# Two-layer diffusion backbone: the last feed-forward weights through the rings, the norm's products in the tokens' place

## The chip, the cores and the metric

One core of a Trainium2 chip runs the whole forward pass in one launch. The metric is the device time in microseconds of one execution; the median of three runs of the kernel before is 2040.7 us (2039.86 to 2040.83). The engines in the rows are TensorE (PE for the matmuls, PEld for its weight loads), VectorE (DVE), ScalarE (ACT), GpSimd (POOL), and SyncE (SP), which starts the transfers.

## What is computed

512 latent tokens and 256 context tokens of 1024 channels pass two layers. Context tokens go through the same steps as latent ones in layer 0. Each layer mixes tokens in two branches (attention over a window of neighbours, and grouped attention over all), then has a gated feed-forward part of 2816 hidden channels. Layer 1, the last, updates latent tokens alone. Cut to what matters:

```python
DEPTH = 2; SEQ = 512; CTX_LEN = 256; D_MODEL = 1024; D_FF = 2816
def swiglu(h, w_in, w_out):
    a, u = jnp.split(h @ w_in, 2, axis=-1)
    return (jax.nn.silu(a) * u) @ w_out
for l in range(DEPTH):
    ...
    h = modulate(rms_norm(x, norm1[l]), sh1, sc1)
    na_q, na_k, na_v, gq, gk, gv, ga, gb = jnp.split(h @ w_in[l], IN_SPLITS, axis=-1)
    ...
    x = x + g1 * branch_merge(ya, yb, ga, gb, w_pa[l], w_pb[l], w_o[l])
    h2 = modulate(rms_norm(x, norm2[l]), sh2, sc2)
    x = x + g2 * swiglu(h2, w_ffn_in[l], w_ffn_out[l])
    ...
return rms_norm(x, final_norm)
```

## The kernel before, in words

Channels lie on the 128 partitions, tokens on the free axis: `x[k]` is channel block k of 8. All is fp32 in value, and each matmul is done as three in fp32r: high part by high part, high by low, low by high (`steps`, L377). So each block of weights is loaded raw (`wr`), rounded on ACT to its high part `wh` (L362), and DVE or POOL subtracts to get the low part `wl` (L364). The ring of raw buffers has four places, those of high and low parts three each; beside them is a pool of 45 slots of 768 columns, "s", for tokens, hidden blocks and much else.

The feed-forward part does most of its products in a scheme of seven in place of eight (`qu`, `qv`, `qc`, L1691). Its last six hidden blocks (`LAST`) come at its end in the plain way: for each of two groups of tokens, for each of eight output blocks j, 6 x 3 = 18 matmuls into `po` (L377), the residual (DVE, L1570: `x[j]` plus gate times `po`), the square of it for the next norm (ACT, L474 for the first and L477) and the addition of squares (DVE, L478). The groups are tokens 0 to 512 and 512 to 768 in layer 0, 0 to 256 and 256 to 512 in layer 1. The hidden block that ends last is `ph`/`pl` (L1777 and L1778). Here the eight blocks of weights, high and low, are kept in 16 of the 45 slots (`kept`) through both groups.

After a group, `done` makes its norm: `st` (L489, sum over partitions on TensorE), `rs` (L498 on DVE, L499 the power on POOL), `rb` (L502, spread to all partitions). In layer 0 `following` then writes the group's tokens to DRAM (`xd`, L1941; layer 1 reads them back for its residual) and makes layer 1's normed input: for each k a product `u` (DVE, L522), its high part `h` (ACT, L523), its low part `hl` (DVE, L524). Context tokens are left for `late_norm`, inside layer 1's mixing. In layer 1 `final` scales and writes the output (L1950 to L1953).

The framework's scheduler sets the order on every engine from these calls; TensorE's is written by hand only in the mixing and in the seven-products part. In mixing, a planner with a clock of its own puts projections among the attention: `PLAN` gives their order as `fill` (`gq` queries, `gb` gates, `nq`, `nk`, `nv` queries, keys and values of the window branch), and until its clock passes `quiet`, a few low parts and rotary products go to DVE rather than POOL. Layer 1 starts with the keys and first queries of the grouped branch, for which two kept blocks are converted in L1263 and L1264 (`kh`, `kl`).

Of the kernel before, what the change touches and what calls it, by code (L numbers as in the profile page):

```python
# [12 lines left out]
F32 = mybir.dt.float32  # L13
# [7 lines left out]
P = 128  # L21
D = 1024
KB = D // P
S = 512
CTX = 256
T = S + CTX
DEPTH = 2
# [6 lines left out]
CHUNK, LAST = 4, 6  # L34
# [8 lines left out]
for _n in ORDER:  # L43
    for _j in range(COLS[_n][1]):
# [25 lines left out]
               "gb4 nk1 gb5 nq2 nk2 nv1 nq3 nk3 gb6 gb7"),  # L70
         early=0.9, reserve=8, hop=0.14, move=3.5, soon=0.5, keep=2,
         busy=12, ctx=0.0, vat=(1, 1), load=2, qt=2, rx=2, slow=(1.1, 1.2, 1), banks="gst", lead=(2, 1, 2), quiet=0.0, spared=0),
    dict(fill=("gq1 gb0 nq0 nv0 gq2 gb1 gq3 gb2 nq1 nk0 gb3",
               "nk1 nk2 nq2 nv1 nk3 gb4 nq3 gb5 gb6 gb7"),
         early=0.8, reserve=2, hop=0.2, move=3, soon=0, keep=2,
         busy=2, ctx=1, vat=(1, 1), load=2.5, qt=2, rx=1, slow=(1, 1, 1), banks="tsg", lead=(2, 2, 1), quiet=18.0, spared=2),
]


# [14 lines left out]
def drain(steps):  # L94

    while True:
        try:
            next(steps)
        except StopIteration as e:
            return e.value  # L100
# [166 lines left out]
class Ops:  # L267
# [6 lines left out]
    def add(self, engine, cost, run, args, after, urgency):  # L274
        self.ops.append((engine, cost, run, args, after, urgency))
        return len(self.ops) - 1
# [51 lines left out]
class Trunk:  # L328
# [27 lines left out]
    def weight(self, src, cols, eng=None, pool=None):  # L356

        nc = self.nc
        raw = self.raw(src, cols)
        tile = lambda tag: (pool or self.wpool).tile([P, cols], F32R, tag="we" if pool else tag, name=self.name(tag))  # L360
        hi = tile("wh")
        nc.scalar.activation(hi, raw, AF.Copy)  # L362
        lo = tile("wl")
        (eng or nc.gpsimd).tensor_tensor(lo, raw, hi[:].bitcast(F32), op=ALU.subtract)  # L364
        if self.flow:
            self.go(("a", cols), ("v" if eng else "g", cols), at=self.flow.clock + self.plan["load"])
        return hi, lo
# [138 lines left out]
    def modulated(self, l, i, x, acc, a, b, h, pool):  # L506

        rb = self.rstd(acc, b - a, pool)
        for k in range(KB):
            self.modulate(l, i, k, x, rb, a, b, h, pool)  # L510

    def modulate(self, l, i, k, x, rb, a, b, h, pool):
        nc = self.nc
        s = int(a >= S)
        if len(h[0]) == k:
            h[0].append(self.slot("h", F32R))
            h[1].append(self.slot("hl", F32R))
        hi, lo = h[0][k], h[1][k]
        u = pool.tile([P, S], F32, tag="u", name=self.name("u"))[:, : b - a]
        g = self.A[l][i][:, s, k : k + 1]  # L520
        sh = self.mod[l][:, s, 24 * i + k : 24 * i + k + 1]
        nc.vector.scalar_tensor_tensor(u, x[k][:, a:b], g, rb[:, : b - a], op0=ALU.mult, op1=ALU.mult)  # L522
        nc.scalar.activation(hi[:, a:b], u, AF.Identity, bias=sh)  # L523
        nc.vector.scalar_tensor_tensor(  # L524
            lo[:, a:b], u, sh, hi[:, a:b].bitcast(F32), op0=ALU.add, op1=ALU.subtract)
# [742 lines left out]
    def late_norm(self, l, h, at):  # L1268

        nc, flow = self.nc, self.flow  # L1270
        x, acc = at.rest
        nb = CTX // P
        yield Until(max(flow.clock + self.plan["ctx"], flow.ring("t")))
        st = self.rstd(acc, CTX, None, True)
        yield nb * 2 * PASS
        t = self.go(("v", nb))
        flow.took("t", t)
        yield Until(self.go(("p", nb + 3), at=t))
        yield Until(flow.ring("t"))
        rb = self.spread(st, nb, Alias(self.small, "hr"))  # L1280
        yield nb * 2 * PASS
        end = flow.clock
        for k in range(KB):
            self.modulate(l, 0, k, x, rb, S, T, h, Alias(self.att, "p"))
            first = self.go(("v", CTX), at=end if k == 0 else None)
            end = self.go(("a", CTX), ("v", CTX), at=first)
        flow.took("t", first)
        self.ready["h"] = end + 2.0
# [450 lines left out]
    def ffn(self, l, right, late, x, spans, groups, nh, done, pool, beside):  # L1739
        nc, d = self.nc, self.d  # L1740
# [80 lines left out]
            beside.pop(0)[1]()  # L1821

        chunk = (FB - LAST) // CHUNK
        kept, slots = [], _Bufs(None, {}, dict(we=self.spool))
        for a, b in groups:
            acc = None
            for j in range(KB):
                if a == 0:
                    kept.append(self.weight(d["wfo"][l, j, :, chunk * CHUNK * P :], LAST * P, nc.vector, slots))
                w = kept[j]  # L1830
                ps = self.ps("a", "po")[:, : b - a]
                drain(self.steps(ps, w, second[chunk], a, b, LAST))
                self.residual(l, 1, ps, x, j, a, b)
                if l == DEPTH - 1 and b == groups[-1][1] and j >= KB - 2:

                    acc = [acc] if j == KB - 2 else acc
                    acc.append(pool.tile([P, S], F32, tag="sq", name=self.name("sq")))
                    nc.scalar.activation(acc[-1][:, : b - a], x[j][:, a:b], AF.Square)
                else:
                    acc = self.square(x[j], a, b, pool, acc)  # L1840
            done(acc, a, b)

    def run(self):
        nc, tc, d = self.nc, self.tc, self.d
        joint = [(0, S), (S, T)]
        self.flow = None
        with (
# [9 lines left out]
            h = ([], [])  # L1857
            with (
# [5 lines left out]
                pool = _Bufs(pool_, dict(rs=1, row=3, more=1, wr=AHEAD), dict(qt=self.spool))  # L1864
                self.constants(cpool)
                at = Front()
                spare = _Bufs(None, {}, dict(qt=self.spool))
                todo = self.prologue(0, h, joint, spare, at)
                self.start(h, pool, todo)
            xd = [self.dpool.tile([P, S], F32, name=f"xd{k}") for k in range(KB)]  # L1870
            for l in range(DEPTH):
                last = l == DEPTH - 1
                spans = joint[:1] if last else joint
                groups = [(0, 256), (256, 512)] if last else joint
# [4 lines left out]
                with (  # L1879
# [2 lines left out]
                    ExitStack() as stack,  # L1882
                ):
                    self.psum = dict(n=psn, a=psa)
                    slots = dict(acc=self.spool, sq=self.spool, u=self.spool)
                    rows, conds = [], stack.enter_context(tc.tile_pool(name=f"c{l}", bufs=1, reuse_waits="tile"))

                    def one(of, n):
# [8 lines left out]
                    with tc.tile_pool(name=f"m{l}", bufs=1, reuse_waits="tile") as pool_:  # L1897
                        pool = _Bufs(pool_, dict(rs=2, qt=5), slots)
# [4 lines left out]
                        x = []  # L1903
# [26 lines left out]
                    h = ([], [])  # L1930
                    at = Front()
                    with tc.tile_pool(name=f"f{l}", bufs=1, reuse_waits="tile") as pool_:
                        own = dict(we=4) if last else {}
                        pool = _Bufs(pool_, dict(own, ws=1, tt=TEMPS, ps=7, rs=2), slots)

                        def following(acc, a, b):
                            if a == S:
                                at.rest = x, acc
                                return
                            for k in range(KB):  # L1940
                                nc.sync.dma_start(xd[k][:, a:b], x[k][:, a:b])  # L1941
                            self.modulated(l + 1, 0, x, acc, a, b, h, pool)

                        def final(acc, a, b):
                            n = b - a
                            rb = self.rstd(acc, n, pool)
                            for k, up in ((0, 2), (2, 5), (5, 8)):
                                o = self.slot("o")[:, : (up - k) * n].rearrange("p (k c) -> p k c", c=n)
                                for i in range(up - k):
                                    nc.scalar.activation(  # L1950
                                        o[:, i], x[k + i][:, a:b], AF.Copy,
                                        scale=self.norms[:, 2 * DEPTH, k + i : k + i + 1])
                                nc.vector.tensor_tensor(  # L1953
                                    o, o, rb[:, :n].unsqueeze(1).to_broadcast([P, up - k, n]), op=ALU.mult)
                                nc.sync.dma_start(d["out"][k:up, :, a:b].rearrange("k p c -> p k c"), o)

                        self.ffn(
                            l, right, late, x, spans, groups, nh, final if last else following, pool, beside)
# [32 lines left out]
class Hidden:  # L1991
# [33 lines left out]
    def done(self):  # L2025
        self.ended(self.f)
# [19 lines left out]
class Alias:  # L2046
# [3 lines left out]
        self.pool, self.tag = pool, tag  # L2050

    def tile(self, shape, dt, tag=None, name=None):
        return self.pool.tile([P, {"p": T, "hr": 16}[self.tag]], dt, tag=self.tag, name=name)


class Front:
# [103 lines left out]
```

## Time and profile before

| | |
|---|---|
| median of three runs | 2040.7 us (2039.86 to 2040.83) |
| the profiled execution | 2036.27 us, span 2034.4 us |
| granted clock, whole span | 0.983 |
| TensorE / DVE / ACT / POOL busy | 96% / 73% / 47% / 11% |
| last quad product of layer 0, of layer 1 ends at | 1097.3 / 1957.4 us |
| first group's output blocks end at | 1162.0 / 2000.4 us |
| second group's output blocks end at | 1178.4 / 2023.7 us |
| layer 1's first two projections end at | 1193.7 us |

Times within the span are from its start. A row of a stretch gives its length, then the busy time of each engine with the number of instructions, the clock that TensorE was granted (1.00 is full) and the transfers' share. "PE po L377 <- ACT wh L362" names a wait: TensorE's matmul into `po` waited for ACT's `wh`. The chain of waits follows the work that ended last back through its releasers.

### The profile page before, as it was taken

To read this page: it belongs to the slowest core of one execution; us is meant where nothing else is said; L and a number is where in the kernel's file an instruction comes from. 1 tells how busy PE (TensorE), PEld (TensorE's weight loads), DVE (VectorE), ACT (ScalarE), POOL (GpSimd) and SP (SyncE) were. 2 spreads that over 40 slices of the span, in tenths; PEclk is the share of its full clock that TensorE was granted. 3 is DMA by queue.
4 is the path that set the end of the run, shared out by engine and by line. 5 is a ranking of instruction groups with operands and counts; after the bars stand their busy time and mean duration, and the time that the engine had idled before them with its cause. 6 is when DMAs were issued, how large, how long until landed. Compare 5 with 4: busy or idle time off the path is not lost.

```text
span 2034.4 us, 31690 instructions
## 1 busy us (share of the span) xinstructions
PE 1951.3 (96%) x12330; PEld 1794.1 (88%) x12330; DVE 1484.2 (73%) x2809; ACT 946.2 (47%) x1838; POOL 224.9 (11%) x131
## 2 busy tenths in 40 slices
PE   8999999999999999999998799999999999999977
PEld 8989999988999989899997678889888988999976
DVE  7468887798769978788573377888564688778753
ACT  5466665632346424233332245665543454554432
POOL 0332222123100000000000012322300000000000
PEclk9999999999999999999999899999999999999987
DMA  8121112244452343454222301112233515323321
GB/s 313 42 68 40 55 58 71 83 155 160 157 185 73 122 138 115 165 173 154 59 71 65 111 32 63 50 42 82 80 113 104 196 66 165 104 94 104 109 68 42
DMA packets 71671, 210.88 MB, mean 104 GB/s; under 512 B 8544, under 2 KB 10720, under 8 KB 71520
## 3 DMA queue, kind: packets, MB, share of 16 engines
q1 hardware_dynamic: 71520, 208.84, 31.0%
q8 instruction: 97, 1.59, 0.3%
q14 instruction: 54, 0.44, 0.1%
HBM read 196.75 MB, written 6.82 MB: 100 GB/s over the span
## 4 chain that ended last, share of the span: by engine, by line
PE 58%; DVE 10%; DMA 4%; ACT 3%; issue 2%; POOL 0%; DVEq 0%; POOLq 0%; ACTq 0%
PE po L377 19%; PE qu L1691 11%; PE pj L377 9%; PE qv L1691 5%; PE pp L377 4%; DMA wr<-wmodT 3%; PE qc L1691 3%; PE pf L377 2%; DVE wr L446 1%; DVE w L1580 1%; PE pv L943 1%; DVE wl L364 1%; PE sc L1026 1%; ACT wh L362 1%; PE y L1062 1%
## 5 line engine op out<-in xcount | busy, mean ns | idle before, releaser
L362 ACT ACTIVATE wh<-wr 128x1024 fp32r<-128x1024 f32 (+2 forms) x211 | 178.0, 846 | 312.0 <-PE po L377 97.9
L1691 PE MATMUL qu<-r,w 128*128 128x384 f32 (+1 forms) x1872 | 293.3, 310 | 2.0 <-ACT tt L1698 1.9
L1691 PEld LDWEIGHTS qu<-r,w 128*128 128x128 f32 x1872 | 279.5, 188 | 6.6 <-ACT tt L1698 6.1
L377 PE MATMUL pj<-h,wh 128*128 128x512 f32 (+1 forms) x704 | 256.4, 366 | 6.1 <-DVE ql L977 2.2
L377 PE MATMUL pj<-hl,wh 128*128 128x512 f32 (+1 forms) x704 | 247.2, 351 | 0.6 <-DVE hl L524 0.4
L377 PE MATMUL pj<-h,wl 128*128 128x512 f32 (+1 forms) x704 | 246.9, 351 | 0.0
L377 PE MATMUL po<-ph,wh 128*128 128x512 f32 (+1 forms) x576 | 208.4, 362 | 33.6 <-ACT wh L362 28.8
L377 PE MATMUL po<-ph,wl 128*128 128x512 f32 (+1 forms) x576 | 206.1, 358 | 3.1 <-DVE wl L364 3.1
L377 PE MATMUL po<-pl,wh 128*128 128x512 f32 (+1 forms) x576 | 204.8, 356 | 0.8 <-DVE pl L1778 0.8
L1579 ACT ACTIVATE w<-wr 128x512 fp32r<-128x512 f32 x234 | 143.5, 626 | 119.3 <-PE qv L1691 26.4
L364 POOL TENSOR_TENSOR wl<-wr,wh 128x1024 fp32r<-128x1024 f32 (+1 forms) x67 | 148.8, 2224 | 387.4 <-ACT wh L362 387.3
L1570 DVE SCALAR_TENSOR_TENSOR x<-po,G,x 128x256 f32<-128x256 f32 (+3 forms) x168 | 98.4, 595 | 119.8 <-PE po L377 119.5
L1580 DVE TENSOR_TENSOR w<-wr,w 128x512 fp32r<-128x512 f32 x234 | 158.3, 686 | 24.2 <-ACT w L1579 22.6
L377 PEld LDWEIGHTS po<-ph,wh 128*128 128x128 f32 x576 | 116.2, 202 | 51.8 <-ACT wh L362 33.9
L364 DVE TENSOR_TENSOR wl<-wr,wh 128x512 fp32r<-128x512 f32 (+2 forms) x144 | 128.3, 894 | 44.6 <-ACT wh L362 39.6
L1691 PE MATMUL qv<-r,w 128*128 128x384 f32 (+1 forms) x936 | 151.3, 310 | 3.4 <-DVE tt L2014 3.3
L377 PEld LDWEIGHTS pj<-h,wh 128*128 128x128 f32 x704 | 133.0, 189 | 22.5 <-ACT h L523 2.6
L377 PEld LDWEIGHTS pj<-h,wl 128*128 128x128 f32 x704 | 133.0, 189 | 17.9
L377 PEld LDWEIGHTS pj<-hl,wh 128*128 128x128 f32 x704 | 133.6, 190 | 16.0 <-DVE hl L524 2.8
L1691 PEld LDWEIGHTS qv<-r,w 128*128 128x128 f32 x936 | 140.8, 189 | 5.3 <-DVE tt L2014 5.3
L499 POOL TENSOR_TENSOR rs<-rs,expo 128x2 f32<-128x2 f32 (+2 forms) x8 | 6.2, 774 | 1187.6 <-DVE rs L498 1187.6
L377 PEld LDWEIGHTS po<-ph,wl 128*128 128x128 f32 x576 | 115.6, 201 | 21.9 <-DVE wl L364 7.8
(242 smaller groups left out, 4294.5 us busy)
## 6 DMA issues: line engine op xcount, KB each, us to landing
wr<-wfi SPq DMA_DIRECT2D x88, 512.0 KB, 3.3
wr<-wmodT SPq DMA_DIRECT2D x86, 512.0 KB, 3.3
wr<-win SPq DMA_DIRECT2D x68, 512.0 KB, 3.2
wr<-wfo SPq DMA_DIRECT2D x64, 256.0 KB, 2.7
wr<-wo SPq DMA_DIRECT2D x26, 512.0 KB, 3.5
wr<-wp SPq DMA_DIRECT2D x32, 256.0 KB, 2.9
x<-x SPq DMA_DIRECT2D x16, 384.0 KB, 7.5
bias<-rpb SPq DMA_DIRECT2D x16, 384.0 KB, 3.0
```

The costliest lines, as they stand in the source:

```text
L362: nc.scalar.activation(hi, raw, AF.Copy)
L364: (eng or nc.gpsimd).tensor_tensor(lo, raw, hi[:].bitcast(F32), op=ALU.subtract)
L377: nc.tensor.matmul(ps[:, : b - a], u[:, c], v[k][:, a:b], start=(k == 0 and i == 0), stop=(k == nk - 1 and i == 2),)
L446: nc.vector.tensor_tensor_reduce(w, w, crow[:, 0], 1.0, 0.0, ALU.mult, ALU.add, self.mod[l][:, 0, n : n + 1])
L499: nc.gpsimd.tensor_tensor(r[:, :nb], r[:, :nb], self.expo[:, :nb], op=ALU.pow)
L943: nc.tensor.matmul(ps[:, t * 256 : t * 256 + 256], a[k][:, tok], b[:, c], start=(k == 0 and i == 0), stop=(k == KB - 1 and i == 2))
L1026: nc.tensor.matmul(s[:, lo:up], qt[:, b * P : (b + 1) * P], kk[k][:, lo:up], start=(k == 0 and (b % 2 == 0 or lo > 0)), stop=(k == 1), ski ...
L1062: nc.tensor.matmul(y[:, 0:256], val[:, k * P : (k + 1) * P], pts[k // 2][hl][:, j * 256 : (j + 1) * 256], start=(hl == 0 and k == 0), stop ...
L1570: self.nc.vector.scalar_tensor_tensor(x[j][:, f:u], ps[:, f - a : u - a], self.G[l][i][:, s, j : j + 1], x[j][:, f:u], op0=ALU.mult, op1=A ...
L1579: nc.scalar.activation(t[:, :n], src, AF.Copy)
L1580: nc.vector.tensor_tensor(t[:, n : 2 * n], src, t[:, :n].bitcast(F32), op=ALU.subtract)
L1691: nc.tensor.matmul(banks[bank], u[:, c], v, start=(first and k == 0 and i == 0), stop=(k == kn - 1 and i == 2), skip_group_check=True)
```

## The change

There are four edits. The last feed-forward weights go through the usual rings instead of kept slots; the second group takes the output blocks from 7 down to 0, reuses what it still finds (7, 6, 5), and loads and converts 4 to 0 again. The write of `xd[j]` is issued right behind the residual of block j in layer 0's first group, rather than for all blocks after it. `modulate` writes its product into `x[k]` itself, so that this waits for the write of `xd[k]`, and no buffer `u` is needed. In `PLAN` for layer 1, `gq2` comes ahead of `nv0`, and `quiet` is 28 for 18. Lines behind `modulate` get one number more (residual L1571, product L523, high part L524, low part L525), those behind the loop two.

```diff
-    dict(fill=("gq1 gb0 nq0 nv0 gq2 gb1 gq3 gb2 nq1 nk0 gb3",
+    dict(fill=("gq1 gb0 nq0 gq2 nv0 gb1 gq3 gb2 nq1 nk0 gb3",
...
-         busy=2, ctx=1, vat=(1, 1), load=2.5, qt=2, rx=1, slow=(1, 1, 1), banks="tsg", lead=(2, 2, 1), quiet=18.0, spared=2),
+         busy=2, ctx=1, vat=(1, 1), load=2.5, qt=2, rx=1, slow=(1, 1, 1), banks="tsg", lead=(2, 2, 1), quiet=28.0, spared=2),
...
-        u = pool.tile([P, S], F32, tag="u", name=self.name("u"))[:, : b - a]
+        u = x[k][:, a:b]
...
-        kept, slots = [], _Bufs(None, {}, dict(we=self.spool))
-        for a, b in groups:
+        ws = {}
+        for i, (a, b) in enumerate(groups):
             acc = None
-            for j in range(KB):
-                if a == 0:
-                    kept.append(self.weight(d["wfo"][l, j, :, chunk * CHUNK * P :], LAST * P, nc.vector, slots))
-                w = kept[j]
+            for at, j in enumerate(list(range(KB))[:: 1 - 2 * i]):
+                if i == 0 or at >= 3:
+                    ws[j] = self.weight(d["wfo"][l, j, :, chunk * CHUNK * P :], LAST * P, nc.vector)
+                w = ws[j]
                 ps = self.ps("a", "po")[:, : b - a]
                 drain(self.steps(ps, w, second[chunk], a, b, LAST))
                 self.residual(l, 1, ps, x, j, a, b)
-                if l == DEPTH - 1 and b == groups[-1][1] and j >= KB - 2:
-                    acc = [acc] if j == KB - 2 else acc
+                if l < DEPTH - 1 and i == 0:
+                    nc.sync.dma_start(self.xd[j][:, a:b], x[j][:, a:b])
+                if l == DEPTH - 1 and i == 1 and at >= KB - 2:
+                    acc = [acc] if at == KB - 2 else acc
...
-                            for k in range(KB):
-                                nc.sync.dma_start(xd[k][:, a:b], x[k][:, a:b])
```

How this moves instructions is seen at three places. First ACT at the end of layer 0, from the high part of the last hidden block (`ph`) on; `x_6223` is block 0, `x_6225` block 1 and so on, `wh` 768 columns wide are the weights of the output blocks. Before:

```order
L1777 ACTIVATE ph_11212<-ph_11119 128x768
L474 ACTIVATE acc_11243<-x_6223 128x512
L362 ACTIVATE wh_11247<-wr_11245 128x768
L477 ACTIVATE sq_11271<-x_6225 128x512
L362 ACTIVATE wh_11276<-wr_11274 128x768
L477 ACTIVATE sq_11300<-x_6227 128x512
L362 ACTIVATE wh_11305<-wr_11303 128x768
L477 ACTIVATE sq_11329<-x_6229 128x512
L362 ACTIVATE wh_11334<-wr_11332 128x768
```

With the change:

```order
L362 ACTIVATE wh_11278<-wr_11276 128x768
L2003 ACTIVATE ph_11119<-tt_11141 128x384
L1778 ACTIVATE ph_11212<-ph_11119 128x768
L362 ACTIVATE wh_11308<-wr_11306 128x768
L362 ACTIVATE wh_11338<-wr_11336 128x768
L362 ACTIVATE wh_11368<-wr_11366 128x768
L474 ACTIVATE acc_11244<-x_6223 128x512
L477 ACTIVATE sq_11273<-x_6225 128x512
L477 ACTIVATE sq_11303<-x_6227 128x512
L362 ACTIVATE wh_11398<-wr_11396 128x768
```

Before, a square stands between any two conversions. Now three conversions follow the hidden block's, and two more stand ahead of it, before the first square (`acc`).

Second, DVE in layer 0's second group, at the norm of layer 1's input. Before:

```order
L522 SCALAR_TENSOR_TENSOR u_11471<-x_6223,A_0_108,rb_11464 128x512
L1570 SCALAR_TENSOR_TENSOR x_6233<-po_11631,G_1_111,x_6233 128x256
L524 SCALAR_TENSOR_TENSOR hl_11470<-u_11471,mod_105,h_11469 128x512
L522 SCALAR_TENSOR_TENSOR u_11477<-x_6225,A_0_108,rb_11464 128x512
L1570 SCALAR_TENSOR_TENSOR x_6235<-po_11654,G_1_111,x_6235 128x256
L524 SCALAR_TENSOR_TENSOR hl_11476<-u_11477,mod_105,h_11475 128x512
L522 SCALAR_TENSOR_TENSOR u_11483<-x_6227,A_0_108,rb_11464 128x512
L1570 SCALAR_TENSOR_TENSOR x_6237<-po_11677,G_1_111,x_6237 128x256
L1264 TENSOR_TENSOR kl_11829<-wr_11825,kh_11827 128x512
```

With the change, from the residual of block 4 of that group on:

```order
L1571 SCALAR_TENSOR_TENSOR x_6231<-po_11583,G_1_111,x_6231 128x256
L364 TENSOR_TENSOR wl_11668<-wr_11664,wh_11666 128x768
L523 SCALAR_TENSOR_TENSOR x_6223<-x_6223,A_0_108,rb_11464 128x512
...
L523 SCALAR_TENSOR_TENSOR x_6237<-x_6237,A_0_108,rb_11464 128x512
L1571 SCALAR_TENSOR_TENSOR x_6229<-po_11612,G_1_111,x_6229 128x256
L525 SCALAR_TENSOR_TENSOR hl_11470<-x_6223,mod_105,h_11469 128x512
L364 TENSOR_TENSOR wl_11697<-wr_11693,wh_11695 128x768
```

Before, product and low part came in turn, with residuals of the second group between. Now the eight products, one for each k, stand in one piece behind the residual of block 4 and the subtraction for block 1; the residual of block 3, the first low part and the subtraction for block 0 (`wl_11697`) come behind them.

Third, DVE at layer 1's end, from the last hidden block's steps on (`x_16002` before and `x_16016` now are block 0). Before:

```order
L2019 TENSOR_TENSOR ph_20237<-ph_20237,tt_20292 128x256
L1778 TENSOR_TENSOR pl_20331<-ph_20237,ph_20330 128x512
L1570 SCALAR_TENSOR_TENSOR x_16002<-po_20341,G_1_113,x_16002 128x256
L364 TENSOR_TENSOR wl_20367<-wr_20363,wh_20365 128x768
L1570 SCALAR_TENSOR_TENSOR x_16004<-po_20369,G_1_113,x_16004 128x256
L478 TENSOR_TENSOR acc_20361<-acc_20361,sq_20389 128x256
L364 TENSOR_TENSOR wl_20396<-wr_20392,wh_20394 128x768
L1570 SCALAR_TENSOR_TENSOR x_16006<-po_20398,G_1_113,x_16006 128x256
```

With the change:

```order
L364 TENSOR_TENSOR wl_20410<-wr_20406,wh_20408 128x768
L2021 TENSOR_TENSOR ph_20251<-ph_20251,tt_20306 128x256
L1779 TENSOR_TENSOR pl_20345<-ph_20251,ph_20344 128x512
L1571 SCALAR_TENSOR_TENSOR x_16016<-po_20355,G_1_113,x_16016 128x256
L1571 SCALAR_TENSOR_TENSOR x_16018<-po_20383,G_1_113,x_16018 128x256
L1571 SCALAR_TENSOR_TENSOR x_16020<-po_20412,G_1_113,x_16020 128x256
L364 TENSOR_TENSOR wl_20439<-wr_20435,wh_20437 128x768
L364 TENSOR_TENSOR wl_20468<-wr_20464,wh_20466 128x768
L364 TENSOR_TENSOR wl_20497<-wr_20493,wh_20495 128x768
```

Before, residual, addition of squares and the next block's subtraction came in turn. Now a subtraction stands ahead of the hidden block's last step, three residuals follow that step, and then three subtractions.

More of the change, by code (lines that the diff above doesn't have):

```diff
@@ L509, in modulated, with modulate @@
         for k in range(KB):
-            self.modulate(l, i, k, x, rb, a, b, h, pool)
-    def modulate(self, l, i, k, x, rb, a, b, h, pool):
+            self.modulate(l, i, k, x, rb, a, b, h)
+    def modulate(self, l, i, k, x, rb, a, b, h):
         nc = self.nc
@@ L1283, in late_norm @@
         for k in range(KB):
-            self.modulate(l, 0, k, x, rb, S, T, h, Alias(self.att, "p"))
+            self.modulate(l, 0, k, x, rb, S, T, h)
             first = self.go(("v", CTX), at=end if k == 0 else None)
@@ L1869, in run @@
                 self.start(h, pool, todo)
-            xd = [self.dpool.tile([P, S], F32, name=f"xd{k}") for k in range(KB)]
+            xd = self.xd = [self.dpool.tile([P, S], F32, name=f"xd{k}") for k in range(KB)]
             for l in range(DEPTH):
@@ L1884, in run @@
                     self.psum = dict(n=psn, a=psa)
-                    slots = dict(acc=self.spool, sq=self.spool, u=self.spool)
+                    slots = dict(acc=self.spool, sq=self.spool)
                     rows, conds = [], stack.enter_context(tc.tile_pool(name=f"c{l}", bufs=1, reuse_waits="tile"))
@@ L2052, in tile @@
     def tile(self, shape, dt, tag=None, name=None):
-        return self.pool.tile([P, {"p": T, "hr": 16}[self.tag]], dt, tag=self.tag, name=name)
+        return self.pool.tile([P, 16], dt, tag=self.tag, name=name)
 class Front:
```

## The prediction

> **What bounds the kernel now.** I read the page first, then the busy time by stretches, then TensorE's waits, then the chain of waits in two stretches, and last single matmuls. From the page:
>
> ```profile
> span 2034.4 us, 31690 instructions
> PE 1951.3 (96%) x12330; PEld 1794.1 (88%) x12330; DVE 1484.2 (73%) x2809; ACT 946.2 (47%) x1838; POOL 224.9 (11%) x131
> L362 ACT ACTIVATE wh<-wr 128x1024 fp32r<-128x1024 f32 (+2 forms) x211 | 178.0, 846 | 312.0 <-PE po L377 97.9
> ```
>
> TensorE is busy 96% of the span, so over most of it there is little to win, and the mean hides where the rest lies. The last row points at a place: the conversions of weights (L362) have 97.9 us of idle time ahead of them that the output matmuls `po` ended. The stretches around the ends of the two layers (us, then busy time of PE, weight load, DVE, ACT, POOL, the granted clock, DMA):
>
> ```profile
> 1097.30:1162.00 64.70, 44.56 (x153) 32.35 (x154) 22.26 (x27) 14.07 (x19) 0.00 (x0) 0.84 0.32 104
> 1162.00:1178.40 16.40, 16.40 (x139) 16.36 (x138) 7.87 (x15) 2.84 (x5) 1.01 (x1) 1.00 0.05 17
> 1178.40:1193.70 15.30, 13.40 (x48) 7.93 (x46) 11.82 (x20) 8.11 (x18) 0.00 (x0) 1.00 0.20 69
> 1193.70:1500.00 306.30, 295.94 (x1955) 265.91 (x1956) 235.01 (x519) 183.88 (x378) 79.41 (x45) 1.00 0.20 63
> 1957.40:2000.40 43.00, 26.16 (x113) 22.50 (x111) 13.25 (x23) 9.09 (x16) 0.00 (x0) 0.67 0.10 28
> 2000.40:2023.70 23.30, 23.29 (x173) 23.29 (x173) 9.71 (x20) 6.19 (x16) 0.70 (x1) 0.87 0.14 47
> ```
>
> 1097.3 is the end of layer 0's last quad product, 1162 the end of the first group's output blocks, 1178.4 that of the second group's, 1193.7 the end of layer 1's first two projections; 1957.4, 2000.4 and 2023.7 are the same points of layer 1's feed-forward. The two first groups are the bad places: TensorE idles 64.70 - 44.56 = 20.1 and 43.00 - 26.16 = 16.8 us, and the clock is 0.84 and 0.67 there. What it waits for (us in all, times, longest), first layer 0, then layer 1:
>
> ```profile
> PE po L377 <- ACT wh L362: 16.0, 7, 2.5
> ...
> PE po L377 <- ACT wh L362: 12.4, 7, 1.8
> ```
>
> Seven waits for seven blocks after the first. Why each conversion is late, the chain of waits says (start, us, what); one cycle of layer 0, then the last hidden block's chain and three rows of a cycle in layer 1:
>
> ```profile
> 1113.89 4.00 PE po L377 x16
> 1117.91 0.76 DVE x L1570
> 1118.70 0.63 ACT sq L477
> 1119.33 0.74 ACT wh L362
> 1120.09 0.97 DVE wl L364
> 1121.11 4.00 PE po L377 x16
> ...
> 1957.62 0.43 DVE tt L2000
> ...
> 1960.39 0.52 PE po L377 x2
> ...
> 1963.64 3.80 PE po L377 x16
> 1967.47 0.50 DVE x L1570
> ...
> 1969.17 0.97 DVE wl L364
> ```
>
> A block's matmuls end; only then come its residual, its square on ACT, the next block's conversion, its subtraction and the next matmuls. The next conversion doesn't need the square: it merely stands behind it on ACT. The loop is serial because of ACT's order.
>
> **The change at layer 0's end.** In the changed order five conversions stand ahead of the first square (the order of ACT above), and three later ones stand among the squares. TensorE runs blocks 0, 1 and 2 without their last hidden block (45 matmuls, 15 of them ahead of the last quad products, as before), then finishes the three. So the wait for the last hidden block, from 1097.30 to 1100.93 in the rows
>
> ```profile
> 1097.30 0.57 DVE tt L2000
> ...
> 1100.93 0.75 PE po L377 x2
> ```
>
> (3.6 us) is covered by the thirty matmuls left of those. The price of a matmul at full clock: 512 columns from two starts, 256 from 16.40 us for 139 = 0.118, with the norm's small ones among them.
>
> ```profile
> 1112.90 0.50 PE L377 MATMUL po<-ph,wh 128*128 128x512 f32 x1 [2.24 <-ACT wh L362]
> ...
> 1114.46 0.39 PE L377 MATMUL po<-pl,wh 128*128 128x512 f32 x1
> 1114.69 0.39 PE L377 MATMUL po<-ph,wl 128*128 128x512 f32 x1
> ...
> 1136.10 0.79 PE L377 MATMUL po<-ph,wh 128*128 128x512 f32 x1 [2.24 <-ACT wh L362]
> ...
> 1138.11 0.63 PE L377 MATMUL po<-pl,wh 128*128 128x512 f32 x1
> 1138.54 0.63 PE L377 MATMUL po<-ph,wl 128*128 128x512 f32 x1
> ```
>
> That is 1114.69 - 1114.46 = 0.23 at full clock and 1138.54 - 1138.11 = 0.43 at the low one. After 1097.3: 8 x 18 - 15 = 129 matmuls of 512 x 0.232 = 29.9; 144 of 256 and 16 small ones x 0.118 = 18.9; the 48 of the first two projections x 0.232 = 11.1. Together 59.9. What stalls I expect:
> - Heads of blocks 3 to 5, whose subtractions follow the last hidden one's on DVE: 0.5, an estimate from 0.97 each against 4.2 us of matmuls a block.
> - Block 4 of the second group. The ring for `wh` has three places, and with 7, 6, 5 reused the place it takes is block 5's, free only after the last reader. Its conversion (0.84) and subtraction (0.97) can't start before; two matmuls (0.24) run in between: 0.84 + 0.97 - 0.24 = 1.6. Blocks 3 to 1 take places freed before, a block or more ahead.
> - The spread of the norm behind POOL's power (1.01 us there, with matmuls of a block put between): 0.4, an estimate. Block 0 of the second group: its subtraction stands behind eight products `x` (L523) and hl's on DVE. The rows
>
> ```profile
> L524 DVE SCALAR_TENSOR_TENSOR hl<-u,mod,h 128x512 fp32r<-128x512 f32 x8 | 6.0, 748 | 3.2 <-ACT h L523 3.2
> L522 DVE SCALAR_TENSOR_TENSOR u<-x,A,rb 128x512 f32<-128x512 f32 x8 | 5.9, 742 | 1.4 <-PE rb L502 1.4
> ```
>
> give 5.9 for the eight, against 2 blocks x 18 x 0.118 = 4.2 of matmuls ahead, plus some 0.5 for a residual: 2.2 us.
> - The first projection, paced by the rest of the hl's: 0.8. In the kernel before, the norm made each of them only once the last was through (x, h, hl in turn), after the second group; now the eight products come early, under its blocks 2 to 0.
>
> Sum 5.5. So 96.4 (64.7 + 16.4 + 15.3) becomes 59.9 + 5.5 = 65.4: **31.0 gained**. Reloading costs 5 DMAs, 5 x 0.84 on ACT and 5 x 0.97 on DVE, which are busy 2.84 and 7.87 of 16.40 us there; both fit, and are the cover gone wrong in a rival below. The loads:
>
> ```profile
> wr<-wfo SPq DMA_DIRECT2D x16, 384.0 KB, 3.1
> ...
> DMA to landing us min/median/max: 2.0/3.7/5.8
> ```
>
> The first row is a load of such a weight (3.1 us to land), the second the writes of `xd`. On SP the first group's eight writes now stand among the reloads, each behind its residual; block 0's reload has three of them ahead, but it is used seven blocks after the last residual. The product written into `x` must wait for the write of the same block. Block 7's write starts as the first group ends and lands at most 5.8 us later; its product comes past the middle of the second group's 17 us. I count both at nothing; were the write in the way, at most its 5.8.
>
> **At layer 1's end.** After 1957.4 there are 16 x 18 - 22 = 266 matmuls of 256, 7 put ahead of the last quad products that run then too, and 8 small ones: 281 x 0.118 = 33.2. Stalls: the last hidden block's chain (2.8 us from 1957.62 to the two matmuls at 1960.39) has a subtraction of 0.97 put between its DVE steps and only 23 x 0.118 = 2.7 of matmuls to cover it: 1.3 (estimate). Block 3's subtraction stands behind three residuals (3 x 0.50) and takes 0.97 itself, less two pairs of matmuls (0.5) and an overlap: 1.6. Block 4 of the second group as above: 1.6. Block 2 of it, since DVE needs 0.97 + 0.50 and an addition of squares a block, close to the 2.1 of its matmuls, and starts late: 1.2 (estimate). Together 5.7, so 66.3 becomes 38.9: **27.4 gained**, of which 16.8 - 5.7 = 11.1 is idle time, the other 16.3 the low clock.
>
> **The clock.** Both sums take the full clock. A gap of 2.24 us was followed by matmuls 0.43 apart at 1136.10, and by ones 0.23 apart at 1112.90: not each gap costs. Eight matmuls at the low rate cost 8 x (0.43 - 0.23) = 1.6. Bounds: nothing, or five remaining stalls above 1 us x 1.8 = 9. I take 4, the middle, since the stalls are shorter than 2.24. The Trainium skill (TensorE: Matmul & The Clock Gate, "Part 1: The HAM clock gate") says that the clock halves after about 3.4 us of idleness; by it the term would be nothing. The trace has the low rate after 2.24 us of idleness, so here it is not the whole story.
>
> **Mixing of layer 1.** Values' block goes one place later, and with the later `quiet` one subtraction moves from POOL to DVE (rows of such a subtraction):
>
> ```profile
> L364 POOL TENSOR_TENSOR wl<-wr,wh 128x1024 fp32r<-128x1024 f32 x8 | 20.1, 2522 | 52.7 <-ACT wh L362 52.7
> L364 DVE TENSOR_TENSOR wl<-wr,wh x1: 1246/1246/1246, 1195.7 to 1195.7; 128x1024 fp32r<-128x1024 f32 x1
> ```
>
> A lone subtraction is 1.2 us earlier or later. TensorE idles 306.3 - 295.9 = 10.4 us of the whole stretch at clock 1.00, in waits of 1.7 us at most for different things, so no more than 10 can be won; a loss is one or two such waits. I take 0, with +-4.
>
> **Sum.** 31.0 + 27.4 - 4 = 54.4 off the profiled execution: 2036.3 - 54.4 = 1981.9. It was 4.4 below the median of 2040.7, so the median goes to **1986**.
>
> **The rivals.**
> (1) *No clock loss.* The gaps stay short and the clock at 1.00 as after 1112.90: 4 less, **1982**. For it: the gap at 1112.90, longer than any stall I expect, was harmless. Against: the one at 1136.10 wasn't. By the skill's rule above it is this case.
> (2) *The reloads stay serial.* If in each second group all five reloaded blocks pay the old loop: layer 0's loop was 1121.11 - 1113.89 = 7.2 against 4.2, so 3.0 each, layer 1's 6.5 against 2.1, so 4.4 each; 5 x 7.4 = 37, less the 5.4 already counted for reloaded blocks: 31.6 more, **2018**. For it: three places are few, and the squares are still on ACT. Against: the places of blocks 3, 2, 1 are freed ahead.
> (3) *The other side: attention of layer 1 becomes the bound.* With values later and one more subtraction on DVE, each softmax would reach TensorE late:
>
> ```profile
> PE tp L1052 <- DVE p L996: 1.8, 3, 0.9
> ...
> PE sc L1026 <- ACT p L1042: 1.3, 2, 0.9
> PE y L1062 <- DVE ptl L1003: 0.5, 2, 0.3
> ...
> L996 DVE TENSOR_SCALAR p<-p,rc x32: 594/620/1960, 1247.6 to 1368.7; 128x768 f32<-128x768 f32 x32
> ```
>
> Each of the 32 items paying the longest of the three waits (0.9 + 0.9 + 0.3 = 2.1) costs 67: **2053**. It decides from 26 items on (54.4 / 2.1). For it: DVE is busy 235 of 306 us. Against: now only 3 of 32 items wait.
> (4) *The change doesn't do what it says:* conversions wait for their places all the same, **2040**.
>
> **How the numbers follow.** Forecast 0.65, (1) 0.2, (2) 0.09, (3) 0.04, (4) 0.02. The range goes from 1974 (no stall but block 4's, clock at full: 8 + 4 less than forecast) to 2001 (clock at its bound, 5 more; mixing 4; half of the 11.2 of stalls again, 6): it holds the forecast and (1). A difference under 0.2%, some 4 us, can't be told from none. Faster 0.94, the same 0.02, slower 0.04.
>
> **What would show it.** Right: the stretch from the last quad product to the two projections near 65 to 70 us, the end of layer 1 near 39 to 44, both with a granted clock above 0.9; the 16.0 and 12.4 us of waits for `wh` down to a few us, and the chain no longer passing from residual by square to conversion. Block 4 of the second group should show a wait of 1 to 2 us for `wh`. Wrong: a clock as low as before in these stretches, waits for `wl` in every block of a second group (2), many waits for `p` in mixing (3), or products that wait for `xd`.

## The result, and the profile after

The changed kernel takes 1980.9 us (median of four, 1976.0 to 1983.7) where the kernel before takes 2040.8: a ratio of 0.970, with an interval of 0.968 to 0.972. The profiled execution took 1982.1 us, with a span of 1980.3 and a granted clock of 0.991.

The stretches that answer to those shown of before (us, then busy time of PE, weight load, DVE, ACT, POOL, the granted clock, DMA): from layer 0's last quad product to the first group's end, the second group, the first two projections, the whole middle of layer 1 up to its last quad product, and its two groups.

```profile
1100.85:1131.30 30.45, 30.44 (x129) 23.83 (x129) 16.29 (x22) 10.20 (x15) 0.00 (x0) 1.00 0.44 139
1131.30:1152.00 20.70, 19.28 (x162) 19.06 (x161) 16.56 (x26) 12.10 (x17) 1.01 (x1) 1.00 0.39 122
1152.00:1163.97 11.97, 11.74 (x50) 8.70 (x49) 11.83 (x20) 6.56 (x15) 0.00 (x0) 1.00 0.57 188
1163.97:1934.96 770.99, 752.02 (x5003) 687.57 (x5002) 564.73 (x1104) 399.64 (x788) 78.26 (x46) 0.99 0.30 95
1934.96:1953.20 18.24, 17.31 (x138) 16.49 (x138) 12.99 (x24) 8.42 (x17) 0.00 (x0) 1.00 0.44 131
1953.20:1969.60 16.40, 16.40 (x140) 16.40 (x140) 11.57 (x21) 9.11 (x19) 0.70 (x1) 1.00 0.28 89
```

TensorE is busy 30.44 of 30.45 us in layer 0's first group, where it was 44.56 of 64.70, and the clock is 1.00 in all five stretches at the ends. The whole span divides as follows; for before, the middle of layer 1 is

```profile
1193.70:1957.40 763.70, 747.06 (x4993) 682.67 (x4993) 567.55 (x1104) 398.76 (x789) 80.80 (x47) 1.00 0.30 95
```

| stretch | before | after | difference |
|---|---|---|---|
| up to layer 0's last quad product | 1097.3 | 1100.9 | +3.6 |
| from there to layer 1's first two projections | 96.4 | 63.1 | -33.3 |
| on to layer 1's last quad product | 763.7 | 771.0 | +7.3 |
| on to the last output block | 66.3 | 34.6 | -31.7 |
| the rest | 10.7 | 10.7 | 0 |
| span | 2034.4 | 1980.3 | -54.1 |

The two ends give 65.0 us, and 10.9 are lost where the sum expected 0, 3.6 of it where nothing was changed. What TensorE's output matmuls and projections wait for at the end of layer 0, then from layer 1's last quad products on (us in all, times, longest):

```profile
PE po L377 <- DVE wl L364: 1.4, 1, 1.4
PE pj L377 <- DVE wl L364: 0.2, 1, 0.2
...
PE po L377 <- ACT wh L362: 0.6, 2, 0.4
PE po L377 <- DVE wl L364: 0.2, 1, 0.2
```

Of the waits of 16.0 and 12.4 us for `wh`, nothing and 0.6 are left. The chain of waits no longer goes from residual by square to conversion. Its longest piece in each layer is one run of matmuls over several blocks; squares are not in it, and DVE's residuals and subtractions only at the last blocks of layer 0's second group and up to block 3 of layer 1's first:

```profile
1111.19 25.19 PE po L377 x127
...
1940.96 14.75 PE po L377 x121
```

### The profile page after: what moved, and what is told of

The parts are those of the page before. It is cut to its first block, busy times and chain, and to the rows that moved or that the text cites. A ratio compares the mean times of both kernels' runs of the same rounds, so it can differ in the third digit from the quotient of the medians.

```text
span 1980.3 us, 31743 instructions
## 1 busy us (share of the span) xinstructions
PE 1931.2 (98%) x12330; PEld 1786.1 (90%) x12330; DVE 1486.1 (75%) x2820; ACT 953.9 (48%) x1848; POOL 222.9 (11%) x130
## 4 chain that ended last, share of the span: by engine, by line
PE 60%; DVE 9%; DMA 4%; issue 3%; ACT 1%; POOL 0%; DVEq 0%; POOLq 0%; ACTq 0%
PE po L377 18%; PE qu L1692 11%; PE pj L377 10%; PE qv L1692 6%; PE pp L377 4%; DMA wr<-wmodT 3%; PE qc L1692 3%; PE pf L377 2%; DVE wr L446 1%; PE pv L944 1%; DMA wr<-wfi 1%; PE sc L1027 1%; PE y L1063 1%; PE tp L1053 1%; DVE w L1581 1%
## 5 line engine op out<-in xcount | busy, mean ns | idle before, releaser
L362 ACT ACTIVATE wh<-wr 128x512 fp32r<-128x512 f32 (+2 forms) x221 | 186.3, 847 | 348.7 <-PE po L377 117.6
L377 PE MATMUL po<-ph,wh 128*128 128x512 f32 (+1 forms) x576 | 197.3, 344 | 1.4 <-ACT wh L362 1.3
L377 PE MATMUL po<-ph,wl 128*128 128x512 f32 (+1 forms) x576 | 196.5, 342 | 1.7 <-DVE wl L364 1.6
L377 PE MATMUL po<-pl,wh 128*128 128x512 f32 (+1 forms) x576 | 195.9, 340 | 0.0
L364 DVE TENSOR_TENSOR wl<-wr,wh 128x512 fp32r<-128x512 f32 (+2 forms) x155 | 138.6, 899 | 37.8 <-ACT wh L362 32.2
L1571 DVE SCALAR_TENSOR_TENSOR x<-po,G,x 128x256 f32<-128x256 f32 (+3 forms) x168 | 98.1, 594 | 72.8 <-PE po L377 72.5
L1003 ACT ACTIVATE pth<-tp 128x512 fp32r<-128x512 f32 x176 | 103.4, 595 | 65.5 <-PE tp L1053 37.9
L1004 DVE TENSOR_TENSOR ptl<-tp,pth 128x512 fp32r<-128x512 f32 x176 | 119.4, 684 | 15.2 <-ACT pth L1003 13.5
```

Source lines behind the costliest of these rows:

```text
L377: nc.tensor.matmul(ps[:, : b - a], u[:, c], v[k][:, a:b], start=(k == 0 and i == 0), stop=(k == nk - 1 and i == 2),)
L1003: nc.scalar.activation(hi, tp, AF.Copy)
L1004: nc.vector.tensor_tensor(lo, tp, hi[:].bitcast(F32), op=ALU.subtract)
L1571: self.nc.vector.scalar_tensor_tensor(x[j][:, f:u], ps[:, f - a : u - a], self.G[l][i][:, s, j : j + 1], x[j][:, f:u], op0=ALU.mult, op1=A ...
```

## The experiments

Times are medians of four or five executions; each set has runs of the kernel before on the same chip (2038.1 to 2038.6 us), and ratios are against those.

| kernel | us | ratio, interval |
|---|---|---|
| first edit alone | 1978.5 | 0.9702, 0.9687 to 0.9716 |
| changed, old plan (first set) | 1977.4 | 0.9702, 0.9686 to 0.9718 |
| before, squares apart, 43 slots | 2017.1 | 0.9897, 0.9883 to 0.9912 |
| before, 43 slots | 2084.1 | 1.0225, 1.0209 to 1.0240 |
| changed (second set) | 1978.1 | 0.9702, 0.9688 to 0.9717 |
| changed, old plan (second set) | 1974.1 | 0.9683, 0.9669 to 0.9698 |
| changed, old fill, new quiet | 1973.8 | 0.9683, 0.9669 to 0.9698 |
| changed, second group forward | 1978.9 | 0.9708, 0.9691 to 0.9725 |
| changed, old plan, own slots for products (third set) | 1977.7 | 0.9699, 0.9686 to 0.9713 |
| changed, old plan (third set) | 1974.9 | 0.9683, 0.9670 to 0.9696 |

**The first edit alone.** The changed kernel with the three other edits undone; what is left against before:

```diff
...
-            for j in range(KB):
-                if a == 0:
-                    kept.append(self.weight(d["wfo"][l, j, :, chunk * CHUNK * P :], LAST * P, nc.vector, slots))
...
+            for at, j in enumerate(list(range(KB))[:: 1 - 2 * i]):
+                if i == 0 or at >= 3:
+                    ws[j] = self.weight(d["wfo"][l, j, :, chunk * CHUNK * P :], LAST * P, nc.vector)
...
```

> Only the first edit: the last weights through the rings, second group reversed; the norm's products in their own slots, the writes of xd after the group and the old plan, as before. Theory A (the whole gain comes from conversions that no longer stand behind squares): the two layer ends give back about 65 us together, and nothing is lost in mixing; 1974 to 1984. Theory B (the products in the tokens' place and the early writes carry part of it, through the start of layer 1): the stretch from the last quad product of layer 0 to the first projections stays over 70 us, and the time is 1988 or more.

It has 1978.5 us: 59.6 off, as much as the whole change (59.9 and 60.3 in its two sets). The time is theory A's. In its profile the two ends are as short as in the changed one, but for the first two projections, which end some 3 us later (66 us after the last quad product, for 63.1; more below). The ends give back some 62 us together, where theory A had 65.

**Squares apart.** Why did conversions stand behind squares? In the kernel before, the high and low parts, the squares and their sum are all taken from the one pool of slots. Here the squares and their sum get three buffers of their own, and the weights stay kept:

```diff
-SLOTS = 45
+SLOTS = 43
...
-                        pool = _Bufs(pool_, dict(own, ws=1, tt=TEMPS, ps=7, rs=2), slots)
+                        pool = _Bufs(pool_, dict(own, ws=1, tt=TEMPS, ps=7, rs=2, acc=1, sq=2), dict(u=self.spool))
```

> The kernel before, with the weights kept in slots as before, but the buffers of squares and of their sum taken out of the shared slots into three of their own, and 43 slots for 45 to make room. Theory A (conversions stood behind squares because both took slots from one full pool, in program order): ACT's conversions come ahead of the squares, both layer ends go to about 60 and 35 us, and the time falls by 55 to 70 us, without one weight loaded twice. Theory B (keeping the weights is itself what makes the loop serial, and only rings release it): the seven waits for wh stay, and the time is within 10 us of 2040.

> The kernel before with 43 shared slots for 45 and nothing else: what the smaller pool costs by itself, as the control of the run with the squares apart. Theory A: the layer ends stay as before (96 and 66 us), and the order of mixing in layer 0 moves a little: 2036 to 2055. Theory B (fewer slots make the layer ends still more serial): over 2055.

Two slots of 768 columns go to make room for three buffers of 512, and that alone costs 46 us (2084.1 against 2038.1). That is past theory A's range, and yet not theory B's mechanism: of 46.3 us in the profiles, 37.8 lie before layer 0's last quad product and 11.5 in the middle of layer 1, while the layer ends take 96.1 and 63.9 us for 96.4 and 66.3. So the squares' own buffers are judged against the control of 43 slots: 2084.1 to 2017.1, 67.0 off. The ends of the two layers in the control, and with the squares apart:

```profile
1135.10:1231.20 96.10, 73.05 (x338) 55.65 (x337) 41.90 (x61) 24.99 (x41) 1.01 (x1) 0.91 0.26 84
2006.40:2070.30 63.90, 47.41 (x284) 43.79 (x284) 22.92 (x41) 15.29 (x32) 0.70 (x1) 0.76 0.12 36
```

```profile
1135.50:1194.00 58.50, 58.30 (x329) 50.01 (x327) 32.67 (x53) 17.26 (x29) 1.01 (x1) 1.00 0.20 68
1971.70:2003.90 32.20, 32.20 (x273) 32.20 (x272) 17.20 (x36) 13.62 (x33) 0.70 (x1) 1.00 0.10 34
```

In the run with squares apart ACT converts all eight blocks, at 1120.6 to 1130.7, ahead of the first square:

```profile
1129.84 0.85 ACT L362 ACTIVATE wh<-wr 128x768 fp32r<-128x768 f32 x1 [0.21 <-DMA wr<-wfo]
...
1146.31 0.63 ACT L474 ACTIVATE acc<-x 128x512 f32<-128x512 f32 x1 [5.70 <-DVE x L1570]
```

So keeping the weights is not what made the loop serial. Weights and squares took slots from one pool, and taking either out of it frees the loop. (That the pool gives its slots out in the program's order is how theory A explains this; no run shows that part by itself.) In layer 1 TensorE then has no idle time at all (32.20 of 32.20), and the end is 2.4 us shorter than with rings, 0.5 of it because four more of its matmuls run ahead of the last quad product. But it goes with the loss of the two slots here, which costs more than that. Theory A's 55 to 70 us hold against the control; against the kernel before, which it named, the gain is 21.0, because it left out the price of the two slots.

**The plan.** The old fill and quiet in the changed kernel, and the old fill with the new quiet:

```diff
-    dict(fill=("gq1 gb0 nq0 gq2 nv0 gb1 gq3 gb2 nq1 nk0 gb3",
+    dict(fill=("gq1 gb0 nq0 nv0 gq2 gb1 gq3 gb2 nq1 nk0 gb3",
...
-         busy=2, ctx=1, vat=(1, 1), load=2.5, qt=2, rx=1, slow=(1, 1, 1), banks="tsg", lead=(2, 2, 1), quiet=28.0, spared=2),
+         busy=2, ctx=1, vat=(1, 1), load=2.5, qt=2, rx=1, slow=(1, 1, 1), banks="tsg", lead=(2, 2, 1), quiet=18.0, spared=2),
```

> The changed kernel with the old plan for layer 1 (values' block in its old place, quiet 18). The stretch of layer 1 from the first projections to the last quad product was 771 us in the profile after against 764 before. Theory A (about 4 us of that is a lower clock that comes and goes, 2 to 3 us is the plan): within 3 us of the changed kernel, with TensorE's idle time in that stretch 2 us lower. Theory B (the plan costs all of it): 6 to 7 us faster than the changed kernel, near 1974.

> The changed kernel itself, as the control of the two runs on the plan on the same chip: 1976 to 1984 by both theories.

> The changed kernel with the old plan of layer 1, beside the control. Theory A (the plan costs what the profiles show as more waits for the softmax and for kk in mixing): 2 to 4 us faster than the control, also in the medians. Theory B (the difference of the two profiles is the clock's play): the medians agree within 1 us.

> The changed kernel with the old order of fill (values' block in its old place), but quiet at 28. Theory A (the place of the values' block is what costs): as the run with the whole old plan, within 1 us. Theory B (the subtraction that quiet moves from POOL to DVE delays the softmax): as the control, within 1 us.

The first set had no control of its own and could not tell. (Against before it showed no difference: 0.9702, as the changed kernel.) In the second, the old plan is 4.0 us faster than the changed kernel (1972.6 to 1974.6 against 1976.3 to 1978.4, no overlap), and the old fill with the new quiet is as fast (1973.8). So the place of the values' block costs, and quiet nothing. A kernel with the values' block one place earlier still, ahead of `nq0`, has no time, because it deadlocks. Whether a still earlier place would gain more stays open. What TensorE waits for in layer 1's mixing (some 240 us from the first projections on), first the changed kernel of this set, then the old plan:

```profile
PE sc L1027 <- ACT p L1043: 2.0, 2, 1.7
PE tp L1053 <- DVE ptl L1004: 1.9, 1, 1.9
...
PE sc L1027 <- DVE kk L1340: 1.4, 1, 1.4
```

```profile
PE pv L944 <- DVE ql L978: 3.1, 2, 2.0
PE tp L1053 <- DVE p L997: 1.9, 3, 0.9
...
PE sc L1027 <- ACT p L1043: 1.2, 2, 0.9
```

Waits of the grouped attention (its scores `sc` and transposes `tp`) come in place of one at the window branch's values (`pv`). All waits listed there are 11.1 against 9.9 us, and the whole middle of layer 1 is 767.2 against 765.2 us, so these two profiles show 2 of the 4 us; they also differ by 3.6 us before layer 0's last quad product, where the kernels are the same. Over the profiles of all sets, the middle takes 767.2 to 771.3 us in the three with the new fill and 765.2 to 767.1 in the four with the old one and the three other edits: 3.4 us between the means, near the 4.0 of the medians. One difference stands in each of them: the spread of a norm (`rb`, L502), some 520 us after layer 0's last quad product, waits 1.5 to 2.1 us for POOL with the new fill and 0.6 to 0.9 with the old, and only with the new fill do 3.4 us at half the clock come with it.

**The second group forward.** All eight blocks are loaded and converted again in each layer.

```diff
-            for at, j in enumerate(list(range(KB))[:: 1 - 2 * i]):
+            for at, j in enumerate(list(range(KB))):
-                if i == 0 or at >= 3:
+                if True:
```

> The changed kernel with the second group in forward order, so that all eight blocks are loaded and converted again. Theory A (places are free in time and the reversal saves only work): DVE has 8 x (0.96 + 0.48 + 0.67) = 16.9 us of work under 17 us of matmuls in layer 0 and as much in layer 1, so it falls behind a little: 3 to 8 us slower than the control. Theory B (the reversal is what keeps the loop from being serial): each reloaded block pays 3 to 4.4 us, 16 blocks some 55 us, near 2035.

1978.9 against 1978.1: a miss of both theories. The ends take 63.1 and 34.7 us, as in the changed kernel, and the same wait of 1.4 us is there. DVE in layer 0's end:

```profile
L364 DVE TENSOR_TENSOR wl<-wr,wh 128x768 fp32r<-128x768 f32 (+1 forms) x17 | 17.0, 1003 | 1.5 <-ACT wh L362 1.5
L1571 DVE SCALAR_TENSOR_TENSOR x<-po,G,x 128x512 f32<-128x512 f32 (+1 forms) x16 | 9.8, 615 | 13.3 <-PE po L377 13.3
```

DVE still idles 13.3 us ahead of residuals in that stretch: my estimate counted the second group alone, and left out that its conversions begin under the first (in this profile two of them run before 1128.6 us, where the first group ends, and a third starts there). So the reversal saves transfers and conversions, but no time.

**The norm's products.** With the old plan, the products in slots of their own again:

```diff
...
-        u = x[k][:, a:b]
+        u = pool.tile([P, S], F32, tag="u", name=self.name("u"))[:, : b - a]
...
```

> The changed kernel with the old plan and with the norm's products in slots of their own again: rings, reversal and early writes of xd stay. To be set beside the changed kernel with the old plan on this chip. Theory A (the products in the tokens' place end the first projections 6 us earlier, and mixing gives back 2 to 4 us, since it waits for other things): 2 to 4 us slower than that. Theory B (all is given back): within 1 us of it.

> The changed kernel with the old plan, as the control of this set: 1972 to 1978 by both theories.

1977.7 against 1974.9: 2.8 us slower (1975.8 to 1980.4 against 1972.6 to 1975.5), as theory A had it. (The first set has a looser pair, the first edit alone and the old plan, which differ in the products and the early writes: 1978.5 and 1977.4, and their executions overlap. So the size is good to some 2 us.) In the profile the products and low parts come in turn again, and a projection waits for them: in the kernel with the first edit alone, whose products stand in the same way,

```profile
1155.17 0.50 PE L377 MATMUL pj<-hl,wh 128*128 128x512 f32 x1 [1.60 <-DVE hl L525]
```

From the last quad product to ACT's second square of the first projections it is 68.1 us there and in this run, and 64.1 with the products in the tokens' place: 4.0 saved. At layer 1's last quad product the profiles of the third set still differ by 3.6 us, the medians by 2.8. For the early writes of `xd`, the kernel with the first edit alone and the one with the products' own slots differ in them alone: 0.9702 and 0.9699 of before, in different sets, so they show no effect.

The fastest here is the changed kernel with the old fill, 1973.8 to 1974.9 us in the second and third sets, 0.968 of before (1977.4, 0.970, in the first).

## Why the prediction was right

The profiled execution was put at 1981.9 us and took 1982.1, the median at 1986 and took 1980.9. The closeness is luck: the two ends gave 65.0 us where the sum had 58.4, the 4 us of lost clock were not lost there, and 10.9 us that the sum didn't have were lost elsewhere. The medians also stand otherwise to the profiles (1.2 us below here, 4.4 above before).

**Layer 0's end: right, 2 us too dear.** 63.1 for 65.4: idle time is 0.01 + 1.42 + 0.23 = 1.7 where I had 5.5 of stalls, and the matmuls took 61.5 for 59.9 (129 of 512 columns in 30.44 is 0.236 each, not 0.232, and the small ones were dearer). Blocks 0 to 2 ran without a gap over the wait for the last hidden block, as put. Block 4 of the second group was to cost 1.6, because its `wh` would take block 5's place. That step failed: the ring gives the place that came free first, and that is block 7's. ACT's conversions of the second group:

```profile
1133.59 0.85 ACT L362 ACTIVATE wh<-wr 128x768 fp32r<-128x768 f32 x1 [0.66 <-PE po L377]
1135.71 0.85 ACT L362 ACTIVATE wh<-wr 128x768 fp32r<-128x768 f32 x1 [1.27 <-PE po L377]
1138.73 0.85 ACT L362 ACTIVATE wh<-wr 128x768 fp32r<-128x768 f32 x1 [2.17 <-PE po L377]
```

Block 7 began at 1131.3 and its 18 matmuls of 0.118 end at 1133.4; the first conversion follows at once, two blocks ahead of its use. So each place is refilled while two other blocks run, and rival (2), the serial reloads, has nothing to stand on. Block 0's subtraction behind the eight products was to cost 2.2 and did cost 1.4:

```profile
1142.65 5.35 DVE L523 SCALAR_TENSOR_TENSOR x<-x,A,rb 128x512 f32<-128x512 f32 x8
1147.91 0.48 DVE L1571 SCALAR_TENSOR_TENSOR x<-po,G,x 128x256 f32<-128x256 f32 x1
1148.31 0.74 DVE L525 SCALAR_TENSOR_TENSOR hl<-x,mod,h 128x512 fp32r<-128x512 f32 x1
1148.97 0.95 DVE L364 TENSOR_TENSOR wl<-wr,wh 128x768 fp32r<-128x768 f32 x1
```

```profile
1149.97 0.39 PE L377 MATMUL po<-ph,wl 128*128 128x256 f32 x1 [1.42 <-DVE wl L364]
```

The mechanism is as put; the term was 0.8 too large. The heads of blocks 3 to 5 and the norm's spread (0.5 and 0.4) cost nothing that shows, and the first projection 0.2 of its 0.8. No product waited for a write of `xd`.

**Layer 1's end: right in its mechanism, 4 us too dear.** 34.6 for 38.9. Where I had 5.7 of stalls, these are all that the profile lists:

```profile
1936.33 0.38 PE L377 MATMUL po<-ph,wl 128*128 128x256 f32 x1 [0.18 <-DVE wl L364]
1939.60 0.39 PE L377 MATMUL po<-ph,wh 128*128 128x256 f32 x1 [0.40 <-ACT wh L362]
1940.34 0.39 PE L377 MATMUL po<-ph,wh 128*128 128x256 f32 x1 [0.23 <-ACT wh L362]
```

Those listed come to 0.8, all idle time to 0.9. 1.6 of the 5.7 was block 4's wrong place again, and nothing shows of block 2's 1.2 behind it. The last hidden block's chain (1.3) shows only as the 0.18 of a subtraction ahead of it. At block 3 I had 1.6 for a subtraction behind three residuals; DVE ran these in 1.27 us, the waits of 0.40 and 0.23 are for conversions, which began when the first three blocks gave their places up, and the subtraction came in time behind them.

**The clock: wrong place.** I took 4 us for stalls that pull the clock down at the ends; it was 1.00 in all five stretches. Rival (1) describes the ends. By the Trainium skill (TensorE: Matmul & The Clock Gate, "Part 1: The HAM clock gate") no gap here is long enough to halve the clock, and at the ends of this profile, with 1.4 us as the longest gap between output matmuls, the trace agrees; with the gaps of 2.24 us in the kernel before it did not always, and in the middle of layer 1 of this same profile it does not. Three waits there (the last number of each row is idle time in us), and the stretches in which the clock was at half:

```profile
1217.93 2.60 PE L1027 MATMUL sc<-kk,q 128*128 128x512 f32 x8 [1.66 <-ACT p L1043]
1310.02 0.70 PE L1053 MATMUL tp<-ident_sb,p 128*128 128x128 f32 x4 [1.91 <-DVE m L1041]
1620.75 0.92 PE L502 MATMUL rb<-ident_sb,rs 128*128 128x128 f32 x4 [1.79 <-POOL rs L499]
```

```profile
1218.34:1221.75 3.41, 3.41 (x15) 3.02 (x14) 2.13 (x6) 2.02 (x5) 0.00 (x0) 0.50 0.00 0
1310.50:1313.91 3.41, 3.41 (x16) 3.22 (x15) 2.43 (x6) 1.32 (x3) 0.00 (x0) 0.50 0.00 0
1607.46:1614.28 6.82, 4.72 (x19) 4.02 (x19) 5.60 (x12) 5.07 (x13) 0.00 (x0) 0.50 0.24 77
1621.11:1624.52 3.41, 3.41 (x19) 3.41 (x18) 2.82 (x8) 2.30 (x7) 0.00 (x0) 0.50 0.35 136
```

These three waits of 1.7 to 1.9 us were each followed, within 0.5 us, by 3.4 us at half the clock; the 1.42 us at layer 0's end was not, nor was a wait of 1.7 us for `kg` at the start of layer 1. And a low stretch need not stand right behind a wait: in the kernel before, one began in the middle of running matmuls, 2.0 us after the end of the wait of 2.24 us ahead of them:

```profile
1129.31:1132.72 3.41, 3.41 (x9) 2.67 (x9) 0.13 (x1) 1.06 (x1) 0.00 (x0) 0.50 0.44 149
```

So the prediction's count by single gaps was too simple; what decides is not shown here. Clock was also lost in the first 40 us, which the change doesn't touch. Before and after:

```profile
0.00:40.00 40.00, 33.50 (x268) 31.88 (x269) 29.21 (x61) 19.49 (x26) 3.09 (x6) 1.00 0.93 360
```

```profile
0.00:40.00 40.00, 33.98 (x251) 33.20 (x252) 26.79 (x59) 19.48 (x26) 3.08 (x6) 0.91 0.90 345
```

0.09 of 40 is the 3.6 us by which layer 0's last quad product came later. That is one execution: over the profiles of kernels that share this stretch it ended between 1096.2 and 1101.3 us.

**Mixing: missed.** I took 0 with 4 to either side. The middle of layer 1 grew by 7.3 us in the profiles. 0.8 of it are the seven matmuls put ahead of the last quad products, which belong to the ends. Of the rest, TensorE's idle time grew by 19.0 - 16.6 = 2.3 us, and its busy time by 4.1 beyond those 0.8. That is the clock: it was at half for 17.1 us in the four stretches above, and before for 6.8 us in all,

```profile
1634.48:1641.31 6.83, 5.52 (x23) 5.19 (x24) 5.58 (x13) 5.04 (x12) 0.00 (x0) 0.50 0.22 77
```

and half of the difference is 5.1 us. The runs on the plan put the price of the values' place at 4.0 us in the medians, at the bound. "One or two such waits" was the right kind of loss, but I gave it no weight in the sum, and left out that a wait can also cost clock behind it. Rival (3) is the same mechanism at all 32 items; in the waits shown above it comes to one or two of them.

**The products in the tokens' place** were not a term of their own: I counted them within the projections. They are worth 2.8 us in the third set. What carries the change is the first edit, 59.6 of 60; the other three come to little, 2.8 won and 4.0 lost, the sum of the parts being as uncertain as these.

**Why conversions stood behind squares** was told only as ACT's order. The runs show what sets that order: buffers from one pool.

## What to carry to other kernels

When an engine's queue alternates between two kinds of work that don't need each other, look for what they share: here, buffers from one pool tied the next weights to the last squares. A move of either to buffers of its own was worth 60 to 67 us here, and can be tried with the smaller of the two; but count what a pool pays for each place taken from it (here 46 us for two of 45). And price a ring by which place comes free first, not by the turn in which places were filled. A wait that is short by itself can cost as much again in clock: here, three times, 1.7 to 1.9 us of waiting and then 3.4 us at half the clock.

## What was not expected

A kernel's stretch that is the same in every version ended 5 us apart between executions (1096.2 to 1101.3 us) with the clock granted in its first 40 us at 0.91 in one and 1.00 in another; differences of 2 or 3 us between single profiles say nothing here, and the plan's 4 us took a control on the same chip. And the three extra reloads a layer of the forward order, each with its conversion and subtraction, cost no time: its ends of 63.1 and 34.7 us are those of the reversed one.
